# A head's queries and keys split by one wide operation per part, in a fused two-layer decoder kernel on one Trainium2 core

## Chip, core and metric

The kernel runs on one core of one Trainium2 chip, in one launch. The metric is the device time of that launch in microseconds. Three runs of the kernel before gave 3035.72, 3030.76 and 3033.51 us, median 3033.51 us.

## What is computed

Two layers over a sequence of 2048 tokens of width 1024. Layer 0 is a gated linear recurrence next to a pooling mixer. Layer 1, in which the change lies, is causal attention with 16 heads of 64, query and key normalisation and a cumulative forget bias. The part of the reference that matters:

```python
q = rms_norm(hd(q), qnorm_g); k = rms_norm(hd(k), knorm_g)
cumf = jnp.cumsum(log_sigmoid(fl + b_f), axis=1)
logits = q @ k.T * scale + cumf[query] - cumf[key]     # per head, causal
probs = softmax(where(mask, logits, -inf))
o = (probs @ v) * silu(g)
```

## The kernel before, in words

The sequence is cut into four segments of 512 tokens (`s` = 0 to 3). For each segment layer 0 runs, then layer 1. Products are made accurate by splitting operands into a rounded high part (fp32r) and the remainder, the low part; a product of two split operands takes the three terms high·high, high·low, low·high.

In layer 1, `quad_attention` (L1207) goes over the heads. For head `h` it runs `attend(s, h)`, 4(s+1) blocks of 128 keys: scores `pst` (L1148, L1149), two exponentials on ScalarE (L1153, L1154), the low part `pl` on VectorE (L184), values `pov` and `pol`. Between these blocks it runs `max_pass(s, h+1)` (L1091), which finds each query's largest score for the next head from products `pmx` (L1100), and writes it as one row of that head's `Q3` (L1114). After a head's blocks, `prep(s, h+2)` (L1059) makes the operands of the head after next. There are 64 calls of `prep`, one per segment and head. Projections of later heads (`pqk`, `pv`, `pgt`) are woven in as filling for TensorE.

`prep` transposes the normalised queries and keys of one head into one PSUM tile `pt` (named pqkT): queries on rows 0 to 63, keys on rows 64 to 127. From it come four operand tiles of 128 rows and 512 columns:

- `Q3` rows 0 to 63: high query; rows 64 to 79: constants from DRAM (`q4d`, L1079), one of which `max_pass` later overwrites with the maximum
- `K2` rows 0 to 63: high key; rows 64 to 79: forget bias from DRAM (`cfd`, L1080)
- `Q1`: high query on the lower rows, low query on the upper; `K1`: low key on the lower, high key on the upper

The scores are K1ᵀQ1 + K2ᵀQ3. `max_pass` needs only `Q3` and `K2`; `attend` needs all four, one head later. For s < 3, `K1` and `K2` are also stored to DRAM (L1082, L1083) for later segments, by the queue of SyncE (SP); weight loads (`raw`, L290) and loads of old keys and values (L1088, L1138, L1141) go through the same queue. The two loads of constants are issued from ScalarE's queue. An issue in an engine's queue that waits for a semaphore holds what stands behind it.

The order of instructions on each engine is set when the program is built: a scheduler takes instructions by priority (nearly the order in the source) when it reckons them ready. Each engine then runs its list strictly in order.

Of the kernel before, what the change touches and what calls it, by code (L numbers as in the profile page):

```python
# [12 lines left out]
AF = mybir.ActivationFunctionType  # L13
ALU = mybir.AluOpType
# [21 lines left out]
def trunk(ctx, tc, x, cvec, norm_g, ada_c, ada_w, ada_b, ada_bg, lbp, w0, w0o, w1, w1f, w1o,  # L36
          onorm, poolw, pscale, foxb, qkg, out):
    nc = tc.nc
    V, S, G = nc.vector, nc.scalar, nc.gpsimd
# [4 lines left out]
    def transpose(o, i):  # L44
        return nc.tensor.transpose(o, i, ident[0:i.shape[0], 0:i.shape[0]])
# [25 lines left out]
    def ps_misc(name):  # L71
        return ps.tile([P, 512], F32, name=name, tag="mx", bufs=2)

    def ps_pj(name):
        return ps.tile([P, 512], F32, name=name, tag="pj", bufs=2)
# [13 lines left out]
    def f(ap):  # L89
        return ap.bitcast(F32)  # L90
# [133 lines left out]

    def need(L, key, fill):
        while key not in L and fill.step():
            pass
        assert key in L, key

# [70 lines left out]
    def next_w(key, ahead=True):  # L300
        n = wpos[0]
        assert wseq[n] == key, (wseq[n], key)
        prep_w(n)
        if ahead:
            prep_w(n + 1)
        wpos[0] += 1
        return wready.pop(n)
# [203 lines left out]
    def hgrn_qf(s, h):  # L511
        L = seg0[s]
        wt, act = next_w(("a", QF[h])), L["act"]
        pq = ps_pj("pq")
        first = s == 0 and h == 0
        if first:
            pf = ps_pj("pf")
            yield from proj_T2((pq, pf), wt, act)
        else:
            yield from proj_T(pq, wt, 0, act)  # L520
        qT = qp.tile([P, SEG], F32, name="qT", tag="qa")
        S.copy(qT, pq)
        yield
        if not first:
            pf = ps_pj("pf")
            yield from proj_T(pf, wt, P, act)
        e1, e2 = tmp("e1"), tmp("e2")
        S.activation(e1, pf, AF.Exp, scale=-1.0)
        S.activation(e2, pf, AF.Exp)
        S.activation(e1, e1, AF.Ln, bias=1.0)  # L530
        S.activation(e2, e2, AF.Ln, bias=1.0)
        S.activation(e1, e1, AF.Exp, scale=-1.0)
        kT = qp.tile([P, SEG], F32, name="kT", tag="qb")
        S.activation(kT, e2, AF.Exp, scale=-1.0)
        V.tensor_scalar(kT, kT, oml[:, h:h + 1], None, op0=ALU.mult)
        S.activation(e1, e1, AF.Ln, scale=oml[:, h:h + 1], bias=lb[:, h:h + 1])
        cT = kp.tile([P, SEG], F32, name="cT", tag="k1c")
        for c in range(NTB):
            V.tensor_tensor_scan(cT[:, c * P:(c + 1) * P], e1[:, c * P:(c + 1) * P],
                                 zero1.to_broadcast([P, P]), 0.0, op0=ALU.add, op1=ALU.add)  # L540
        L["qkc", h] = (qT, kT, cT)
        yield
# [515 lines left out]

    def prep(s, h):  # L1059

        L = seg1[s]
        qk = L["qk", h // 2]
        j = h % 2
        pt = ps_misc("pqkT")
        for tb in range(NTB):
            transpose(pt[:, tb * P:(tb + 1) * P], qk[:, tb, j * P:(j + 1) * P])
        lo, up = slice(0, HD), slice(HD, P)
        g = col["qkg"]
        Q1 = qp.tile([P, SEG], F32R, name="Q1", tag="qa")
        Q3 = qp.tile([P, SEG], F32R, name="Q3", tag="qb")  # L1070
        K1 = kp.tile([P, SEG], F32R, name="K1", tag="k1c")
        K2 = kp.tile([P, SEG], F32R, name="K2", tag="k2c")
        S.activation(Q1[lo], pt[lo], AF.Copy, scale=g[lo])
        S.activation(K1[up], pt[up], AF.Copy, scale=g[up])
        V.scalar_tensor_tensor(Q1[up], pt[lo], g[lo], f(Q1[lo]), op0=ALU.mult, op1=ALU.subtract)
        V.scalar_tensor_tensor(K1[lo], pt[up], g[up], f(K1[up]), op0=ALU.mult, op1=ALU.subtract)
        S.copy(Q3[lo], f(Q1[lo]))  # L1077
        S.copy(K2[lo], f(K1[up]))
        nc.scalar.dma_start(f(Q3[HD:KX]), q4d)  # L1079
        nc.scalar.dma_start(f(K2[HD:KX]), cfd[h, :, s * SEG:(s + 1) * SEG])  # L1080
        if s < NSEG - 1:
            nc.sync.dma_start(k1d[h, :, s * SEG:(s + 1) * SEG], f(K1))  # L1082
            nc.sync.dma_start(k2d[h, :, s * SEG:(s + 1) * SEG], f(K2[0:KX]))  # L1083
        L["ops", h] = (Q1, Q3, K1, K2)
# [122 lines left out]
    def quad_attention(s, quad, fill):  # L1207

        L = seg1[s]
        nb = NTB * (s + 1)  # L1210
        for h in range(4 * quad, 4 * quad + 4):
            nxt = max_pass(s, h + 1) if h + 1 < NH else iter(())
            next(nxt, None)
            need(L, ("v", h // 2), fill)
            if h > 0 and h % 2 == 0:
                need(L, ("g", (h - 1) // 4), fill)
            for i, _ in enumerate(attend(s, h)):
                if i < nb - 2:
                    next(nxt, None)
                if i == nb // 2:  # L1220
                    next(nxt, None)
                if i == 0 and h > 0:
                    finish(s, h - 1)
                yield
            run(nxt)
            if h + 2 < NH:
                need(L, ("qk", h // 2 + 1), fill)
                prep(s, h + 2)

    def layer1(s, xs):  # L1230
# [10 lines left out]
        vq = v_quad(s, 0, ("c", 1))  # L1241
        next(vq)
        prep(s, 0)
        next(vq)
        prep(s, 1)

        fill = Steps()
# [140 lines left out]
```

## Time and profile before

| | us |
|---|---|
| runs | 3035.72, 3030.76, 3033.51 |
| median | 3033.51 |
| profiled execution, its own time | 3029.48 |
| its span, first to last instruction | 3027.8 |
| mean granted TensorE clock | 0.975 |

The profile gives, for one execution, each engine's busy time, the chain of waits that ended last, and every instruction with its line, its tiles and the idle time of its engine before it. PE is TensorE, PEld its weight loads, DVE VectorE, ACT ScalarE, POOL GpSimd, SP SyncE (which only issues transfers). A small q behind an engine means its sequencer. Tile numbers are left out, so `Q<-pqkT` at L1073 is the write of `Q1`, and at L1077 `Q<-Q` the copy into `Q3`.

### The profile page before, as it was taken

What the parts mean: (1) busy time and instruction counts of PE and PEld (TensorE: products, weight loads), DVE (VectorE), ACT (ScalarE), POOL (GpSimd) and SP (SyncE); (2) the same over time, 40 slices, a digit from 0 to 9 for tenths busy, and PEclk for the clock granted to TensorE, in tenths of its full rate; (3) what the DMA queues carried; (4) which work ended last, traced back from release to release, by engine and by line L of the source; (5) the groups of instructions that cost most, each with busy time, mean ns of one, the idle gap of its engine ahead of it and who ended that gap; (6) DMA issues with size and microseconds to landing.
All of it is one profiled execution on the core that took longest, in us unless ns stands there. A gap on an engine that the chain in (4) does not pass through costs nothing.

```text
span 3027.8 us, 49244 instructions
## 1 busy us (share of the span) xinstructions
PE 2808.9 (93%) x17212; PEld 2390.2 (79%) x17212; DVE 2301.3 (76%) x4390; ACT 1826.4 (60%) x3743; POOL 1172.5 (39%) x992
## 2 busy tenths in 40 slices
PE   4699999989999999989999999998999999999998
PEld 3688887879888887868878887776898877777777
DVE  8667678776676788886586788889667678888886
ACT  3344566774445666775455676768635467777774
POOL 3111233323211444444212355554432136566665
PEclk9899999999999999999999999999999999999999
DMA  7523365534233444533333443553342334333442
GB/s 246 174 57 102 106 141 139 119 91 124 79 102 110 119 119 104 131 99 115 100 95 116 122 124 115 126 133 113 97 126 71 114 104 115 105 113 107 113 138 86
DMA packets 207888, 348.97 MB, mean 115 GB/s; under 512 B 24068, under 2 KB 70788, under 8 KB 205080
## 3 DMA queue, kind: packets, MB, share of 16 engines
q1 hardware_dynamic: 201816, 329.03, 39.0%
q10 hardware_dynamic: 5824, 16.79, 1.7%
q8 instruction: 137, 2.24, 0.3%
q14 instruction: 111, 0.91, 0.1%
HBM read 293.58 MB, written 52.14 MB: 114 GB/s over the span
## 4 chain that ended last, share of the span: by engine, by line
PE 60%; DVE 19%; ACT 11%; DMA 4%; issue 4%; POOL 1%; SPq 0%; ACTq 0%; DVEq 0%; POOLq 0%
PE py L42 10%; PE pgt L42 8%; PE pqk L42 8%; PE pst L42 6%; PE pv L42 6%; PE pmx L42 4%; PE pov L42 3%; PE pol L42 3%; PE pf L42 3%; PE pq L42 3%; PE pl L42 3%; DVE pl L184 2%; DVE wt L184 2%; ACT wt L295 1%; DMA raw<-in_w_dram 1%
## 5 line engine op out<-in xcount | busy, mean ns | idle before, releaser
L184 POOL TENSOR_TENSOR wt<-raw,wt 128x512 fp32r<-128x512 f32 x287 | 419.5, 1470 | 1030.9 <-ACT wt L295 975.1
L1164 POOL TENSOR_TENSOR la<-la,ph 128x512 f32<-128x512 f32 (+3 forms) x528 | 610.6, 1156 | 385.7 <-ACT ph L1153 342.9
L184 DVE TENSOR_TENSOR pl<-pst,ph 128x512 fp32r<-128x512 f32 (+3 forms) x640 | 386.9, 605 | 133.4 <-ACT pst L1154 102.2
L1153 ACT ACTIVATE ph<-pst 128x512 fp32r<-128x512 f32 (+3 forms) x640 | 340.6, 532 | 235.1 <-PE pst L42 224.9
L42 PE MATMUL pqk<-wt,h 128*128 128x256 f32 x3072 | 433.1, 286 | 5.5 <-DVE h L497 2.7
L42 PEld LDWEIGHTS pqk<-wt,h 128*128 128x128 f32 x3072 | 411.9, 192 | 25.2 <-DVE h L497 3.5
L42 PE MATMUL pgt<-h,wt 128*128 128x512 f32 x1536 | 403.9, 405 | 0.0
L295 ACT CAST wt<-raw 128x512 fp32r<-128x512 f32 x578 | 335.2, 621 | 74.9 <-PE py L42 33.3
L42 PE MATMUL pv<-wt,h 128*128 128x256 f32 x2304 | 345.0, 298 | 10.7 <-DVE h L184 6.6
L42 PEld LDWEIGHTS pv<-wt,h 128*128 128x128 f32 x2304 | 326.1, 204 | 28.9 <-DVE h L184 9.6
L42 PEld LDWEIGHTS pgt<-h,wt 128*128 128x128 f32 x1536 | 293.1, 194 | 63.2 <-issue 1.9
L1154 ACT ACTIVATE pst<-pst 128x512 f32<-128x512 f32 (+3 forms) x640 | 340.0, 531 | 0.0
L184 DVE TENSOR_TENSOR wt<-raw,wt 128x512 fp32r<-128x512 f32 x291 | 265.7, 918 | 73.4 <-ACT wt L295 71.9
L1102 DVE TENSOR_REDUCE mxs<-pmx 128x1 f32<-128x512 f32 x384 | 258.6, 684 | 20.3 <-PE pmx L42 17.2
L42 PE MATMUL py<-wt,o 128*128 128x256 f32 x1536 | 202.2, 286 | 1.4 <-ACT o L1200 1.2
L42 PE MATMUL py<-wt,mix 128*128 128x256 f32 x1536 | 198.2, 287 | 2.3 <-DVE yt L844 2.1
L42 PEld LDWEIGHTS py<-wt,o 128*128 128x128 f32 x1536 | 192.8, 192 | 6.7 <-ACT o L1200 1.5
L42 PEld LDWEIGHTS py<-wt,mix 128*128 128x128 f32 x1536 | 187.9, 191 | 9.8 <-issue 4.5
L42 PE MATMUL pst<-Q,K1o 128*128 128x512 f32 x384 | 162.6, 424 | 23.2 <-DVE pl L184 21.7
L42 PE MATMUL pmx<-K2o,Q 67*128 67x512 f32 x384 | 162.0, 426 | 21.9 <-ACT Q L1077 10.2
L42 PE MATMUL pov<-ph,Vo 128*128 128x512 f32 x384 | 162.8, 425 | 6.6 <-ACT ph L1153 6.2
L1104 DVE CUSTOM_DVE_ANT_0 pmx<-pmx,mq 128x128 f32<-128x128 f32 (+3 forms) x256 | 124.6, 497 | 55.6 <-PE pmx L42 53.8
(251 smaller groups left out, 5309.1 us busy)
## 6 DMA issues: line engine op xcount, KB each, us to landing
raw<-in_w_dram SPq DMA_DIRECT2D x448, 256.0 KB, 3.5
K2o<-k2d SPq DMA_DIRECT2D x192, 160.0 KB, 3.4
Vo<-vd SPq DMA_DIRECT2D x96, 260.0 KB, 2.7
K1o<-k1d SPq DMA_DIRECT2D x96, 256.0 KB, 3.4
raw<-in_w1o_dram SPq DMA_DIRECT2D x66, 256.0 KB, 3.6
raw<-in_w0o_dram SPq DMA_DIRECT2D x64, 256.0 KB, 3.2
vd<-Vc SPq DMA_DIRECT2D x48, 260.0 KB, 8.1
ada<-in_ada_w_dram ACTq DMA_DIRECT2D x12, 1024.0 KB, 5.0
```

The source lines that it names most:

```text
L42: return nc.tensor.matmul(*a, **k)
L184: (eng or V).tensor_tensor(out_t, full, f(hi), op=ALU.subtract)
L295: S.copy(wt[:, 0, sl, :], raw)
L1102: V.tensor_reduce(mxs[:, i, c:c + 1], pm[:, 0:n], axis=AX.X, op=ALU.max)
L1104: V.tensor_tensor_reduce(pm[:, 0:n], pm[:, 0:n], mq[:, SEG - n:], 1.0, NEG, op0=ALU.add, op1=ALU.max, accum_out=mxs[:, i, c:c + 1])
L1153: S.activation(ph[:, q0:], st[:, q0:], AF.Exp)
L1154: S.activation(st[:, q0:], st[:, q0:], AF.Exp)
L1164: G.tensor_tensor(la[:, q0:], la[:, q0:], f(ph[:, q0:]), op=ALU.add)
```

## The change

Only `prep` changes, and its instructions stand one line lower from L1074 on.

```diff
-        S.activation(Q1[lo], pt[lo], AF.Copy, scale=g[lo])
-        S.activation(K1[up], pt[up], AF.Copy, scale=g[up])
-        V.scalar_tensor_tensor(Q1[up], pt[lo], g[lo], f(Q1[lo]), op0=ALU.mult, op1=ALU.subtract)
-        V.scalar_tensor_tensor(K1[lo], pt[up], g[up], f(K1[up]), op0=ALU.mult, op1=ALU.subtract)
-        S.copy(Q3[lo], f(Q1[lo]))
-        S.copy(K2[lo], f(K1[up]))
+        S.activation(Q3, pt, AF.Copy, scale=g)
+        V.scalar_tensor_tensor(Q1, pt, g, f(Q3), op0=ALU.mult, op1=ALU.subtract)
+        nc.sync.dma_start(f(K1[lo]), f(Q3[up]))
+        S.copy(K2[lo], f(Q3[up]))
+        S.copy(K1[up], f(Q1[up]))
+        S.copy(Q1[up], f(Q3[lo]))
         nc.scalar.dma_start(f(Q3[HD:KX]), q4d)
         nc.scalar.dma_start(f(K2[HD:KX]), cfd[h, :, s * SEG:(s + 1) * SEG])
```

One wide activation (now L1074) writes the high parts of query and key into the two halves of `Q3`, one wide VectorE operation (L1075) the low parts into `Q1`. The high key goes to `K1`'s lower rows by a transfer from SP's queue (L1076) and to `K2` by a copy (L1077); the low key is copied to `K1`'s upper rows (L1078), and only then the high query over it to `Q1`'s upper rows (L1079). The `q4d` rows (now L1080) overwrite rows 64 to 79 of `Q3`, on which the high key stood, so that load now waits for the transfer and the copy that read them. `Q1` and `K1` hold their parts on swapped rows, and their product is the same.

ScalarE's queue around the `prep` of segment 1, head 9. The tiles of that head are `Q1_12458`, `Q3_12459`, `K1_12460` and `K2_12461`; `ph` and the second `pst` are exponentials, `lh` and `wt` copies of other work. Before:

```order
L1079 DMA Q3_12459<-q4d_175 16x512
L1153 ACTIVATE ph_12427<-pst_12423 128x128
L1154 ACTIVATE pst_12423<-pst_12423 128x128
L1114 ACTIVATE Q3_12168<-pmt_12447 1x512
L1175 COPY u_12147<-pov_12188 64x512
L1073 ACTIVATE Q1_12458<-pqkT_12453,c_qkg_513 64x512
L1074 ACTIVATE K1_12460<-pqkT_12453,c_qkg_513 64x512
L1180 CAST lh_12443<-la_12187 128x512
L1077 CAST Q3_12459<-Q1_12458 64x512
L1078 CAST K2_12461<-K1_12460 64x512
L1080 DMA K2_12461<-cfd_174 16x512
L1153 ACTIVATE ph_12490<-pst_12487 128x512
```

With the change:

```order
L1074 ACTIVATE Q3_12459<-pqkT_12453,c_qkg_513 128x512
L295 CAST wt_12524<-raw_12525 128x512
L1181 CAST lh_12443<-la_12187 128x512
L1077 CAST K2_12461<-Q3_12459 64x512
L1078 CAST K1_12460<-Q1_12458 64x512
L1154 ACTIVATE ph_12490<-pst_12487 128x512
L1079 CAST Q1_12458<-Q3_12459 64x512
L1080 DMA Q3_12459<-q4d_175 16x512
L1155 ACTIVATE pst_12487<-pst_12487 128x512
L295 CAST wt_12524<-raw_12529 128x512
```

The `q4d` load has moved from ahead of the activation to behind all the copies, with the second exponential of a block directly behind it.

TensorE's list at the same place, from the end of that head's transposes (`pqkT`) to its first `pmx`; `pgt` is filling. Before:

```order
L45 MATMUL pqkT_12453<-ident_85,qk_11629 128x128
L42 MATMUL pst_12487<-Q1_12167,K1o_12481 128x512
L42 MATMUL pst_12487<-Q3_12168,K2o_12483 128x512
L42 MATMUL pgt_12541<-h1_9560,wt_12215 128x512 x9
L42 MATMUL pmx_12475<-K2o_12473,Q3_12459 128x512
```

With the change:

```order
L45 MATMUL pqkT_12453<-ident_85,qk_11629 128x128
L42 MATMUL pst_12487<-Q1_12167,K1o_12481 128x512
L42 MATMUL pst_12487<-Q3_12168,K2o_12483 128x512
L42 MATMUL pgt_12541<-h1_9560,wt_12215 128x512 x12
L42 MATMUL pst_12554<-Q1_12167,K1o_12481 128x512
L42 MATMUL pst_12554<-Q3_12168,K2o_12483 128x512
L42 MATMUL pov_12479<-ph_12490,Vo_12485 128x512
L42 MATMUL pgt_12541<-h1_9560,wt_12215 128x512 x10
L42 MATMUL pst_12566<-Q1_12167,K1o_12481 128x512
L42 MATMUL pmx_12475<-K2o_12473,Q3_12459 128x512
```

The first `pmx` has moved behind 28 matmuls where 11 stood before; over the 64 heads the median goes from 22.5 to 49 (matmuls of 256 or 512 columns).

SP's queue at the same place, with the change; before, the store L1082 stood directly behind the load `Vo`:

```order
L1142 DMA Vo_12753<-vd_173 128x520
L1076 DMA K1_12460<-Q3_12459 64x512
L1084 DMA k2d_172<-K2_12461 80x512
L1083 DMA k1d_171<-K1_12460 128x512
L290 DMA raw_12767<-in_w1_dram 128x512
```

The new transfer stands in the place of the store, and the two stores follow it.

## Rows read from the trace of the kernel before

**Rows 1.** The page: busy time by engine, and the chain that ended last.
```profile
PE 2808.9 (93%) x17212; PEld 2390.2 (79%) x17212; DVE 2301.3 (76%) x4390; ACT 1826.4 (60%) x3743; POOL 1172.5 (39%) x992
...
PE 60%; DVE 19%; ACT 11%; DMA 4%; issue 4%; POOL 1%; SPq 0%; ACTq 0%; DVEq 0%; POOLq 0%
```

**Rows 2.** Waits of PE, whole span: for whom, us in total, times, longest.
```profile
PE pst L42 <- DVE pl L184: 35.1, 31, 2.4
...
PE pmx L42 <- ACT Q L1077: 10.2, 19, 1.5
...
PE pmx L42 <- DVE K L1076: 4.2, 8, 0.8
...
PE pmx L42 <- DMA K<-cfd: 2.9, 1, 2.9
...
PE pmx L42 <- ACT K L1074: 2.2, 2, 1.8
...
PE pmx L42 <- ACT K L1078: 1.4, 7, 0.2
```

**Rows 3.** The compute lines of `prep`: duration in ns min/median/max, first and last start.
```profile
L1073 ACT ACTIVATE Q<-pqkT,c_qkg x64: 662/682/687, 370.2 to 2942.1; 64x512 fp32r<-64x512 f32 x64
...
L1075 DVE SCALAR_TENSOR_TENSOR Q<-pqkT,c_qkg,Q x64: 743/744/746, 372.1 to 2943.6; 64x512 fp32r<-64x512 f32 x64
...
L1076 DVE SCALAR_TENSOR_TENSOR K<-pqkT,c_qkg,K x64: 754/755/757, 374.2 to 2944.4; 64x512 fp32r<-64x512 f32 x64
...
L1077 ACT CAST Q<-Q x64: 612/620/624, 372.1 to 2943.5; 64x512 fp32r<-64x512 f32 x64
```

**Rows 4.** Two stretches of attention: length, busy us (and count) by engine, granted clock, DMA share.
```profile
core 0: us, PE busy (x) PEld busy (x) DVE busy (x) ACT busy (x) POOL busy (x), PEclk, DMA share, GB/s
1189.00:1215.00 26.00, 23.32 (x108) 17.45 (x107) 23.91 (x40) 17.84 (x38) 10.68 (x9) 0.93 0.30 93
2076.00:2107.00 31.00, 27.04 (x155) 20.65 (x154) 29.46 (x60) 27.24 (x60) 16.01 (x13) 1.00 0.42 124
```

**Rows 5.** Timeline of the `prep` of segment 1, head 9, and after it.
```profile
1187.00 0.28 PE L45 MATMUL pqkT<-ident,qk 128*128 128x128 f32 x1
...
1187.71 2.23 PE L42 MATMUL pgt<-h,wt 128*128 128x512 f32 x9
1187.94 0.68 ACT L1073 ACTIVATE Q<-pqkT,c_qkg 64x512 fp32r<-64x512 f32 x1
1187.99 0.68 DVE L1177 TENSOR_TENSOR u<-pov,u 64x512 f32<-64x512 f32 x1
...
1189.36 0.62 ACT L1180 CAST lh<-la 128x512 fp32r<-128x512 f32 x1
...
1190.55 0.50 PE L42 MATMUL pmx<-K2o,Q 67*128 67x512 f32 x1 [0.61 <-ACT Q L1077]
...
1191.16 0.60 ACT L1153 ACTIVATE ph<-pst 128x512 fp32r<-128x512 f32 x1
...
1201.82 1.01 PE L42 MATMUL pst<-Q,K 128*128 128x512 f32 x2 [2.07 <-DVE pl L184]
```

**Rows 6.** From issue to landing: the `q4d` load (L1079), then the store of `K1` (L1082, 256 KB).
```profile
L1079 ACTq DMA_DIRECT2D Q<-q4d x64: 308/308/335, 244.2 to 2938.8; - x64
...
DMA to landing us min/median/max: 1.7/2.6/4.5
...
L1082 SPq DMA_DIRECT2D k1d<-K x48: 319/326/420, 375.0 to 2111.2; - x48
L1082 SPq EVENT_SEMAPHORE  x45: 17/4657/11694, 375.0 to 2101.6; - x45
...
DMA to landing us min/median/max: 2.3/2.6/4.4
```

**Rows 7.** The SP queue's own waits: for whom, us in total, times, longest.
```profile
SPq L1082 <- DVE K L1076: 246.2, 40, 11.7
```

## The prediction

> **What bounds the kernel now.** I read the busy times first [rows 1]. TensorE is busy 93% of the span, VectorE 76%, ScalarE 60%; the chain that ended last is 60% TensorE, 19% VectorE, 11% ScalarE. So time can only be won where TensorE stands idle, and lost where it is made to.
>
> The waits of TensorE come second [rows 2]. Its largest wait in attention is for VectorE's `pl`: 35.1 us in 31 waits. Its waits for `prep` itself, at the first `pmx` of a head, are 10.2, 2.2 and 1.4 us for ScalarE's part, 4.2 for VectorE's and 2.9 for the `cfd` rows: 20.9 us in 37 waits.
>
> Third, stretches of attention [rows 4]. In 1189 to 1215 us VectorE is busy 23.91 of 26 us (92%) and TensorE 23.32; in 2076 to 2107 us, where little filling is left, VectorE has 29.46 of 31 us (95%), ScalarE 27.24 and TensorE 27.04. There VectorE is as much the bound as TensorE, unlike over the whole span. The timeline of one head shows it [rows 5]: the transposes of `prep` end at 1187.28 us, the first `pmx` waits 0.61 us at 1190.55 us, and at 1201.82 us TensorE has stood 2.07 us because VectorE is late with `pl`.
>
> **The change part by part.**
>
> *VectorE.* One operation of two goes. By [rows 3] L1075 takes 744 ns and L1076 755 ns on 64 rows and 512 columns. The wide one has the same columns on 128 rows; on ScalarE a copy of 128 rows takes 0.62 us (L1180) [rows 5] and one of 64 rows 0.62 us (L1077) [rows 3], so I price it by the columns, at 0.75 us. VectorE loses 64 × 0.755 = 48.3 us. What of it is on the path: VectorE stands in the chain for 19% of 3027.8 = 575 us, of 2301.3 us busy, a quarter; 48.3 / 4 = 12 us. Ends: nothing, if `pl` is late for other reasons, and 31 waits for `pl` × 0.755 = 23 us, one operation off each. I take −12.
>
> *ScalarE.* Before: 2 × 0.682 + 2 × 0.620 = 2.60 us a head. Now 0.682 + 3 × 0.620 = 2.54 us. 64 × 0.06 = 4 us less; ScalarE has 40% idle, so I count nothing.
>
> *The first `pmx`.* Here the path gets longer. Before, `Q3` was complete after two activations, one other copy and one copy, and its `q4d` rows had been loaded beforehand. Now those rows are loaded last. In the order shown ScalarE has seven instructions ahead of that issue, the wide activation first: 0.68 + 6 × 0.61 = 4.35 us. Over all 64 heads it is five to nine, 3.1 to 5.5 us by these durations, median 4.35. The load then takes 2.6 us to land (1.7 to 4.5) [rows 6]. So `Q3` is ready 4.35 + 2.6 = 7.0 us after the activation starts, which for this head is 1187.94 + 7.0 = 1194.9 us. TensorE in the new order has between the transposes and that `pmx` 22 `pgt` at 2.23 / 9 = 0.25 us [rows 5] and six others at about 0.25: 28 × 0.25 = 7.0 us, so from 1187.28 it arrives at about 1194.3 to 1194.6, if the `pov` among them, which waits for the later exponential, costs some tenths. The wait is 0.3 to 0.6 us, against 0.61 before. So the move of `pmx` by 17 matmuls pays for the longer path, and I count no change for this term. Ends: all 20.9 us vanish if the loads land in 1.7 us; and if half the loads land at the longest, 4.5 us instead of 2.6, 32 × 1.9 = +61 us.
>
> The Trainium skill, SBUF — State Buffer, section The DMA setup-cost knee, says that every transfer pays about 2 us whatever its size, plus its bytes over 436 GB/s. As an estimate from that page the `q4d` load of 32 KB would land in 2.1 us, each `pmx` would be ready 0.5 us earlier, and this term would be about −20 us; the trace's median is 2.6 us, and the sum keeps it.
>
> *The transfer of the high key.* It is issued from SP when the wide activation ends, at 0.7 us, and lands 2.6 us later (2.3 to 4.4), by the store of `K1`, twice its size [rows 6]: at 3.3 us. The `q4d` issue comes up at 4.35 us, so ScalarE does not stand for it, unless landing takes over 4.35 − 0.7 = 3.6 us. SP must be there in time: before, it stood at the store of `K1` for a median of 4.66 us a wait, 246.2 us in all [rows 6, 7], so it was early, and the new transfer has the store's place. In segment 3, where there was no store, SP now waits too, with loads of old keys behind it, but only until the activation is done. Nothing for this, with +6 us as the other end (16 heads × 0.4).
>
> *The new wait of ScalarE for VectorE* (L1078 needs the low part). The low part can start at 0.7 us and end at 1.45; in the head shown VectorE is first done with `u` at 1188.67 [rows 5], 0.73 after the start, so nothing is lost. ScalarE comes to L1078 after 2.4 us at the median. Behind it stand exponentials. Nothing, if VectorE is not over 1 us behind.
>
> *Where filling is short.* In 7 heads near the ends of segments the new order has only 11 to 25 matmuls ahead of the first `pmx`, some 3 us against 7.0 ready. But these are stretches like 2076 to 2107 us, where TensorE has 4 us idle anyway. At most 7 × 4 = 28 us; I take +2.
>
> *The sum.* −12 + 0 + 0 + 2 = −10 us. On the profiled execution, 3029.48 us, that is 3019.5; its time lies 4.0 us under the median of the runs, so for a median I forecast 3033.51 − 10 = **3023.5 us**. The forecast's own range is 3008 to 3029.
>
> **The rivals.**
>
> *1. The first `pmx` comes late (slower).* Two transfers now stand one behind the other ahead of it, and a late `Q3` also holds the `pst` behind that `pmx` on TensorE. It decides where the load's landing exceeds 2.6 us by more than the slack of nothing to 0.3 us. For it: half the loads land later than 2.6 us, up to 4.5 [rows 6], and these are loads that nothing waited for. Against: TensorE has 7.0 us of other work there. Price: between 64 × 0.5 = 32 and 61 us, less the 12 won: 3033.5 + 20 to + 49, at the middle 3068 us.
>
> *2. ScalarE stands at its own queue (slower).* It waits for VectorE at L1078 or for the transfer at the `q4d` issue, and the exponentials behind are late. In the trace before, ScalarE's queue never held a load on a transfer just issued. The Trainium skill, DMA: Bandwidth & Descriptors, section Anatomy of one DMA, says that the DMA engines wait on no semaphore: the issuing sequencer does, ahead of dispatch; no row here shows such a hold on ScalarE, and by that rule the hold would be ScalarE's. If the landing takes 4.4 us [rows 6], it holds 0.8 us a head, 51 us of ScalarE in all. By ScalarE's 11% of the chain 6 us of that are on the path, and if a third of it is, since exponentials stand right behind, 17 us. Against the 12 won that is 3028 to 3039, about 3036 us.
>
> *3. VectorE's work was cover (no change).* The 48 us sit beside TensorE's filling and only move idle time. For it: TensorE has 93% and the same matmuls remain. Against: the 35.1 us of waits for `pl`. Then 3033 us.
>
> *4. More than forecast (faster).* The later `pmx` also moves its maxima on VectorE out of the crowded start of a head. All 35.1 us of the waits for `pl` go: 3033.5 − 35 = 2998 us.
>
> **How the numbers follow.** A measurement of this kernel can tell about 0.2%, 6 us. Forecast 0.38, rival 4 0.12, rival 3 0.18, rival 1 0.22, rival 2 0.10. Faster by over 0.2% is the forecast and rival 4: 0.50. Within 0.2%: rival 3 and part of rival 2: 0.21. Slower: rival 1 and the rest of rival 2: 0.29. The range goes from 2999 (rival 4's end) to 3066, about the middle of rival 1, and leaves out some 2 in 10.
>
> **What would show it.** Right: VectorE busy about 48 us less, with 64 wide operations of about 0.75 us at L1075; the wait of `pst` for `pl` down from 35.1 us towards 20; TensorE's wait at `pmx` for the `q4d` rows about 20 us in all; almost no hold of ScalarE at L1080. Rival 1: a wait of `pmx` for the `q4d` load of 1 us or more a head. Rival 2: long semaphore rows on ScalarE's queue at L1078 or L1080, and waits of TensorE for exponentials above what they are now. The forecast is wrong if the wait for `pl` stays at 35 us, or if the wide VectorE operation takes much over 0.75 us.

## The result, and the profile after

The change made the kernel slower. Four runs of it gave 3068.91 to 3082.71 us, median 3075.68, and four of the kernel before 3030.76 to 3037.74, median 3034.61: a ratio of 1.0138, 95% interval 1.0119 to 1.0158. That is 41 us more, where 10 us less were forecast. The profiled execution took 3076.22 us, its span is 3074.5 us, and its mean granted TensorE clock is 0.969 (before 0.975).

The page of the changed kernel, busy time and chain:

```profile
PE 2823.8 (92%) x17212; PEld 2395.1 (78%) x17212; DVE 2233.3 (73%) x4326; ACT 1826.5 (59%) x3743; POOL 1166.3 (38%) x992
...
PE 56%; DVE 16%; ACT 13%; DMA 9%; issue 4%; POOL 1%; SPq 0%; ACTq 0%; DVEq 0%; POOLq 0%
```

Against [rows 1], VectorE has 68 us less to do and leaves part of the chain, 19% to 16%. What enters it are transfers: 4% to 9%. TensorE makes the same 17212 matmuls, but is busy 14.9 us longer, and its idle time (span less busy) grows from 218.9 to 250.7 us, by 31.8. Both together are the 46.7 us between the two spans.

The lines of `prep` with the change, by line (ns min/median/max, first and last start), with the landing of the two transfers:

```profile
L1074 ACT ACTIVATE Q<-pqkT,c_qkg x64: 663/689/697, 372.3 to 2987.6; 128x512 fp32r<-128x512 f32 x64
...
L1075 DVE SCALAR_TENSOR_TENSOR Q<-pqkT,c_qkg,Q x64: 731/750/753, 373.0 to 2988.9; 128x512 fp32r<-128x512 f32 x64
...
L1076 SPq DMA_DIRECT2D K<-Q x64: 461/467/527, 373.0 to 2988.3; - x64
...
  ACT junk L457: 7.4, 2
  ACT pst L1155: 4.9, 4
...
DMA to landing us min/median/max: 2.2/2.2/3.8
...
L1080 ACTq DMA_DIRECT2D Q<-q4d x64: 308/314/385, 375.3 to 2990.6; - x64
L1080 ACTq EVENT_SEMAPHORE  x58: 17/17/3146, 378.3 to 2990.3; - x58
...
DMA to landing us min/median/max: 1.7/1.9/4.3
```

Every duration came out as priced: 0.75 us for the wide VectorE operation, 0.69 for the wide activation. The two rows of ScalarE under L1076 are idle times that the transfer ended (us, times); with four smaller ones they are 20.7 us. The landing rows look harmless, but the view found a landing for only some of the issues (28 of the 64 `q4d` loads, 17 of the 64 transfers; in [rows 6] 17 of 64 loads), and the timelines below show longer ones. The `q4d` load went out a median of 3.2 us after the activation began, where 4.35 were forecast: 0.7 us to the transfer's issue, 2.2 to its landing, and the load right behind.

The waits of TensorE with the change (for whom, us in total, times, longest):

```profile
PE pov L42 <- ACT ph L1154: 31.9, 38, 3.5
...
PE pst L42 <- DVE pl L184: 20.8, 37, 1.4
PE pst L42 <- DMA K2o<-k2d: 19.8, 13, 3.7
...
PE pmx L42 <- DVE mxs L1103: 12.0, 23, 1.8
PE pmx L42 <- DMA Q<-q4d: 11.6, 8, 6.1
...
PE pmx L42 <- DMA vd<-Vc: 5.4, 1, 5.4
```

The same view of the kernel before, beyond what stands in [rows 2]:

```profile
PE pov L42 <- ACT ph L1153: 8.0, 13, 2.2
...
PE pmx L42 <- DVE mxs L1102: 2.0, 2, 1.5
...
PE pst L42 <- DMA K2o<-k2d: 1.2, 2, 1.0
```

The wait for `pl` fell from 35.1 us [rows 2] to 20.8, as foretold. The waits for exponentials (+23.9), old keys (+18.6), maxima (+10.0) and the `q4d` load (+11.6) are what came. The wait of 5.4 us put down to `vd<-Vc` is that of the first `pmx` of head 12, which reads no v; the `q4d` load of that head had been issued 9.3 us before it ended.

Where in the program? I took the time from the end of one head's transposes to the next's, for all 64 calls of `prep` (numbered 0 to 63, 16 to a segment), and subtracted before from after. About half of the heads became a little faster. Heads 4, 8 and 12 of segments 0 to 2, each the first of a group of four, lost 47.0 us together (numbers 4, 12, 28, 36 and 40 each 7.3 to 9.0), and the nine heads behind them won 16.3 back. Segment 3 lost 11.2 us, where neither kernel stores v. Ahead of and in those nine heads `v_quad` (L1047 to L1049) sends four stores of v to DRAM through SP's queue. These heads are not the whole of it, and not all of their loss is that of the late `pmx`: the version of experiment 7, which has neither the transfer nor the late load and is faster than before, loses 22.2 us in the same nine heads, where loads of old keys come late. Against the version of experiment 1, which differs from the change by the transfer alone, the change loses 20.6 us in the nine heads and those behind them, and 26.7 us in all the others. These are differences of single executions, and the time of the kernel before alone differs by 7 us among its four runs.

Head 4, in segment 0, shows the late load most clearly. A timeline with the change (start, us, engine, line, and in brackets the idle time before):

```profile
446.08 0.60 PE L45 MATMUL pqkT<-ident,qk 128*128 128x128 f32 x4
...
448.14 0.69 ACT L1074 ACTIVATE Q<-pqkT,c_qkg 128x512 fp32r<-128x512 f32 x1
...
448.86 0.47 SPq L1076 DMA_DIRECT2D K<-Q  x1
...
450.14 1.06 SPq L1049 DMA_DIRECT2D vd<-Vc  x2
...
452.03 0.33 SPq L1083 DMA_DIRECT2D k1d<-K  x1
...
452.10 0.32 ACTq L1080 DMA_DIRECT2D Q<-q4d  x1
...
461.29 0.80 PE L42 MATMUL pmx<-K,Q 67*128 67x128 f32 x2 [6.09 <-DMA Q<-q4d]
```

The transfer of the high key was issued 0.7 us after the activation began and the `q4d` load at 4.0 us, near the 4.35 forecast. But the load then took 9.2 us to let `pmx` start: 461.29 − 452.10. In the kernel before, the same head's transposes began at 443.44 us, and its first `pmx` waited 0.21 us:

```profile
448.24 0.33 PE L42 MATMUL pmx<-K,Q 67*128 67x128 f32 x1 [0.21 <-ACT K L1078]
```

What the DMA engines did from 444 to 463 us with the change (busy tenths in 40 slices; then issues: count, KB each, median us to landing):

```profile
DMA  6951000980003898999999799999899999999999
...
vd<-Vc SPq DMA_DIRECT2D x4, 260.0 KB, 8.8
...
k1d<-K SPq DMA_DIRECT2D x1, 256.0 KB, 9.4
```

From the issues at 450.14 us on they are busy in nine tenths of nearly every slice, with four stores of v ahead of or beside the `q4d` load and weight loads of 256 and 512 KB behind it; the store of `K1` issued next to it, at 452.03 us, took 9.4 us, against a median of 2.6 [rows 6].

Head 12 looks the same. In segments 1 and 2 it is the transfer that is late. Head 4 of segment 2, number 36, has two stores ahead of it (the same view):

```profile
1791.53 0.92 SPq L1049 DMA_DIRECT2D vd<-Vc  x2
...
1793.98 0.69 ACT L1074 ACTIVATE Q<-pqkT,c_qkg 128x512 fp32r<-128x512 f32 x1
...
1794.69 0.47 SPq L1076 DMA_DIRECT2D K<-Q  x1
...
1800.00 0.36 ACTq L1080 DMA_DIRECT2D Q<-q4d  x1
1800.03 0.32 SPq L1083 DMA_DIRECT2D k1d<-K  x1
...
1800.41 0.58 ACT L1155 ACTIVATE pst<-pst 128x512 f32<-128x512 f32 x1 [1.75 <-DMA K<-Q]
...
1801.02 0.69 DVE L184 TENSOR_TENSOR pl<-pst,ph 128x512 fp32r<-128x512 f32 x1 [3.92 <-ACT pst L1155]
...
1802.42 0.73 PE L42 MATMUL pmx<-K2o,Q 67*128 67x512 f32 x2
```

The `q4d` load and the store of `K1`, which both wait for the transfer, go off at the same moment, 5.3 us after its issue; ScalarE stands 1.75 us at its own queue, VectorE 3.92 us for the exponential behind it. The first `pmx` comes 8.4 us after the activation. At the six such heads of segments 1 and 2 `q4d` is issued 5.7 to 8.4 us after the activation (median of all heads 3.2); the first `pmx` then waits for it at two of them, 1.3 and 0.5 us. What this costs at numbers 36 and 40 is not shown: the version of experiment 7 loses 6.8 and 7.3 us there too, with waits of 5.0 us each for old keys.

At head 4 the idle time was followed by a lower clock. Two stretches there, ahead of the wait and behind it (length, busy us by engine, then granted clock, DMA share, GB/s):

```profile
446.70:455.00 8.30, 7.68 (x60) 6.92 (x59) 6.50 (x12) 8.10 (x17) 3.79 (x4) 1.00 0.76 151
461.30:467.80 6.50, 6.50 (x28) 5.96 (x29) 4.97 (x13) 1.62 (x4) 0.65 (x2) 0.50 0.61 173
```

TensorE worked at 2.4 GHz, stood idle for 6.09 us, and then had 1.2 GHz for the whole next stretch. By the mean granted clocks of the two executions (0.975 of 3027.8 us, 0.969 of 3074.5) 1.2 GHz was granted for an estimated 40 us more in the changed kernel, which fits the 14.9 us of longer busy time. What head 4 lost did not last: before, the `pmx` at head 5 waited 2.9 us for `cfd` [rows 2] with a lower clock around it, and heads 4 and 5 together took 41.6 us before and 41.8 with the change. Head 12 with the one behind it kept 7.2 us, number 28 with its follower 7.0.

### The profile page after: what moved, and what is told of

The parts are those of the page before. It is cut to its first block, busy times and chain, and to the rows that moved or that the text cites. A ratio compares the mean times of both kernels' runs of the same rounds, so it can differ in the third digit from the quotient of the medians.

```text
span 3074.5 us, 49203 instructions
## 1 busy us (share of the span) xinstructions
PE 2823.8 (92%) x17212; PEld 2395.1 (78%) x17212; DVE 2233.3 (73%) x4326; ACT 1826.5 (59%) x3743; POOL 1166.3 (38%) x992
## 4 chain that ended last, share of the span: by engine, by line
PE 56%; DVE 16%; ACT 13%; DMA 9%; issue 4%; POOL 1%; SPq 0%; ACTq 0%; DVEq 0%; POOLq 0%
PE py L42 9%; PE pgt L42 8%; PE pqk L42 6%; PE pst L42 6%; PE pv L42 4%; PE pov L42 3%; PE pmx L42 3%; PE pol L42 3%; PE pf L42 3%; PE pq L42 3%; PE pl L42 2%; DMA K<-Q 2%; DMA raw<-in_w_dram 2%; DMA K2o<-k2d 2%; ACT wt L295 2%
## 5 line engine op out<-in xcount | busy, mean ns | idle before, releaser
L184 POOL TENSOR_TENSOR wt<-raw,wt 128x512 fp32r<-128x512 f32 x287 | 413.2, 1447 | 1036.7 <-ACT wt L295 981.0
L1154 ACT ACTIVATE ph<-pst 128x512 fp32r<-128x512 f32 (+3 forms) x640 | 341.6, 534 | 250.7 <-PE pst L42 239.5
L42 PE MATMUL pqk<-wt,h 128*128 128x256 f32 x3072 | 442.4, 287 | 5.6 <-DVE h L497 2.6
L42 PEld LDWEIGHTS pqk<-wt,h 128*128 128x128 f32 x3072 | 418.5, 194 | 26.8 <-DVE h L497 3.4
L42 PE MATMUL pv<-wt,h 128*128 128x256 f32 x2304 | 336.6, 293 | 8.4 <-DVE h L184 4.9
L42 PEld LDWEIGHTS pv<-wt,h 128*128 128x128 f32 x2304 | 316.9, 199 | 25.9 <-DVE h L184 7.4
L42 PEld LDWEIGHTS py<-wt,mix 128*128 128x128 f32 x1536 | 187.9, 191 | 11.6 <-issue 4.5
L42 PE MATMUL pst<-Q,K2o 67*128 67x512 f32 x384 | 161.0, 423 | 22.4 <-DMA K2o<-k2d 19.8
L42 PE MATMUL pmx<-K2o,Q 67*128 67x512 f32 x384 | 155.6, 429 | 16.1 <-DVE mxs L1103 10.6
```

The lines of the kernel that those rows point to most:

```text
L42: return nc.tensor.matmul(*a, **k)
L184: (eng or V).tensor_tensor(out_t, full, f(hi), op=ALU.subtract)
L1154: S.activation(ph[:, q0:], st[:, q0:], AF.Exp)
```

## The experiments

Theory A: the first `pmx` is late, because the transfer and then the `q4d` load stand one behind the other ahead of it and both get slow beside the stores of v. Rival B: ScalarE's queue, held at L1080, makes exponentials late. Rival C: the later load alone does it, with or without a transfer. Rival D: the transfer costs by being there, on SP's queue and on the DMA engines. Ratios are to the kernel before, run on the same chip beside each.

**1. No transfer** (against the change):

```diff
-        nc.sync.dma_start(f(K1[lo]), f(Q3[up]))
+        S.copy(K1[lo], f(Q3[up]))
```

> The changed kernel with the high key moved to K1 by a ScalarE copy instead of the transfer; the q4d load still comes last. Theory T (what costs the 41 us are the two transfers that now stand one behind the other ahead of a head's first pmx: at the first head of each quarter of the heads in segments 0 to 2 they queue behind the stores of v, land in 5 us or more, hold ScalarE at the q4d issue, and pmx comes late): no hold at the q4d issue is left, about half the loss goes, 3050 us (3040 to 3060), with waits of pmx for q4d left over. Rival F (the cost is the longer path itself: pmx stands behind twice the filling, which is then missing elsewhere, wherever the transfers land): the path is as long, 3070 us or more. Rival S (ScalarE's longer chain of copies and its wait for VectorE delay the exponentials): one copy of 0.62 us more a head, 3080 to 3110 us.

Measured: 3028.90 us, ratio 1.0016 (0.9999 to 1.0032). A ScalarE copy in place of the transfer takes away nearly the whole loss, though ScalarE has 64 copies more and `q4d` is still loaded after them, a median of 2.5 us after the activation starts (3.2 with the change). On that chip this is 5 us over the kernel before, just under the 6 to 26 that theory T gave, and far from F and S. So the loss of the change goes with its transfer; a late load issued at 2.5 us alone doesn't carry it. The waits of TensorE here:

```profile
PE pst L42 <- DMA K2o<-k2d: 13.2, 13, 2.9
...
PE pov L42 <- ACT ph L1154: 12.6, 19, 2.4
...
PE pmx L42 <- DMA Q<-q4d: 9.6, 5, 2.9
```

The waits for exponentials fall from 31.9 to 12.6 us, but the nine heads with stores of v still lose 21.7 us, with waits for `q4d` and for old keys.

**2. The transfer kept, off the path to `pmx`** (against before: a tile `H` of their own for the high parts, so that the `q4d` rows are loaded early again):

```diff
+        H = tmp("H", F32R)
+        S.activation(H, pt, AF.Copy, scale=g)
+        V.scalar_tensor_tensor(Q1, pt, g, f(H), op0=ALU.mult, op1=ALU.subtract)
+        S.copy(Q3[lo], f(H[lo]))
+        S.copy(K2[lo], f(H[up]))
+        nc.sync.dma_start(f(K1[lo]), f(H[up]))
+        S.copy(K1[up], f(Q1[up]))
+        S.copy(Q1[up], f(H[lo]))
```

> The changed kernel with the high parts in a tile of their own, from which Q3, K2, K1 (still by the transfer) and Q1 are filled, so that the q4d load can be issued ahead of everything again. One ScalarE copy more a head (40 us of ScalarE in all). Theory T: nothing waits for the transfer any more before the next head, no hold, pmx early: 3020 to 3035 us, at or below the kernel before. Rival F: the path is short again, also 3020 to 3035 us. Rival S: 3085 us or more, since ScalarE has more to copy than in the changed kernel.

Measured: 3035.33 us, ratio 1.0041 (1.0029 to 1.0053). The first `pmx` comes a median of 2.26 us after the activation starts (6.88 with the change, 2.73 before), and two thirds of the loss are gone. That is 11 us over the kernel before on that chip, where T and F expected next to none. In its trace numbers 36 and 40 lose 6.9 and 7.0 us, with waits of 4.6 and 4.8 us for old keys.

**3. The transfer from ScalarE's queue** (against the change):

```diff
-        nc.sync.dma_start(f(K1[lo]), f(Q3[up]))
+        nc.scalar.dma_start(f(K1[lo]), f(Q3[up]))
```

> The changed kernel with the transfer issued from ScalarE's queue instead of SP's, so that it stands behind no store or load of SP's queue. Theory T, where the queueing is in SP's own queue: the transfer lands in 2.2 us at every head, the holds at the q4d issue go, 3040 to 3055 us. Theory T, where the sixteen DMA engines themselves are full of the stores of v: landing stays 5 us at those heads, 3070 to 3080 us. Rivals F and S: no change from the changed kernel, 3075 us.

Measured: 3055.48 us, ratio 1.0115 (1.0084 to 1.0146). Standing behind the stores on SP's queue is at most a small part of it; the first `pmx` is nearly as late as with the change, 6.76 us. The result lies between the two expected for theory T, so how much is SP's queue and how much the DMA engines stays open.

**4. A late load without a transfer** (against before: the activation that makes `Q3` also writes its rows 64 to 79, so that `q4d` must follow it; those values are overwritten):

```diff
-        S.copy(Q3[lo], f(Q1[lo]))
+        S.activation(Q3[0:KX], pt[0:KX], AF.Copy, scale=g[0:KX])
```

> The kernel before (two narrow VectorE operations, no transfer) with one thing altered: Q3's activation also writes the rows of q4d, with values that the load then overwrites, so the q4d load has to come after it. Theory T: one load on the path instead of two transfers, no hold of ScalarE; a few heads where the load lands late: 3040 to 3055 us. Rival F: pmx has to be put behind more filling, and VectorE has both its operations: 3065 to 3090 us. Rival S: nothing new on ScalarE, 3035 us.

Measured: 3105.19 us, ratio 1.0277 (1.0249 to 1.0306). It was not the clean test that I wanted: the scheduler put this activation late, behind VectorE's reading of the same PSUM tile, as the row of that line in the by-line view shows, and the first `pmx` came a median of 8.51 us after the first activation.

```profile
L1077 ACT ACTIVATE Q<-pqkT,c_qkg x64: 667/683/687, 376.4 to 3021.7; 80x512 fp32r<-80x512 f32 x64
its engine sat idle before it (us, times) until:
  DVE K L1076: 9.5, 13
```

None of the three expectations came. It shows that a late load can go with a loss of 2.8% without any transfer between tiles. That the lateness itself is what is paid for is likely, taken with experiment 1, but not shown: this edit also makes the activation at L1077 a reader of the PSUM tile and holds that tile longer. A late load that is issued at 2.5 us, as in experiment 1, is early enough at most heads.

**5. The `q4d` load from SP's queue** (against the change), which takes the hold at L1080 off ScalarE:

```diff
-        nc.scalar.dma_start(f(Q3[HD:KX]), q4d)
+        nc.sync.dma_start(f(Q3[HD:KX]), q4d)
```

> The changed kernel with the q4d load issued from SP's queue instead of ScalarE's: it waits for the transfer there, and ScalarE never stands for it. If ScalarE's hold (some 16 us in all in the changed kernel, at a few heads) and the late exponentials behind it are the larger part of the loss: +15 to +25 us against the kernel before. If the late landing of what pmx needs is the larger part: +35 to +45 us, since the load comes no earlier. Rival F: +40 us.

Measured: 3080.42 us, ratio 1.0160 (1.0122 to 1.0198): no gain, and a little more than the 45 us expected at most. So B is not what decides: the hold of ScalarE at heads like number 36 is real, but with the load moved to SP's queue, which now stands for it instead, the waits of TensorE for exponentials only fall from 31.9 to 23.7 us, the first `pmx` comes hardly earlier, a median of 6.71 us after the activation against 6.88, and `pmx` waits longer for `q4d` than with the change, 15.4 us against 11.6.

**6. The stores of v spread out**, with the change and, as a control, in the kernel before. The loop at L1047 to L1049 goes, and each head stores its own v in the middle of its blocks, after GpSimd has written its column of ones once more (that only makes the store wait until then):

```diff
+                    if s < NSEG - 1:
+                        vj = L["v", h // 2][:, :, h % 2, :]
...
+                        nc.sync.dma_start(vd[h, :, s * NTB:(s + 1) * NTB, :], f(vj))
```

> The changed kernel, with each head's store of v issued in the middle of that head (the column of ones is written again from a value of that block, so that the store cannot go earlier) instead of four stores together at the end of a projection, which in the changed kernel fall on the first prep of a quarter. Theory T (the transfer and the q4d load queue behind those stores): against the kernel before, +0 to +15 us instead of the changed kernel's +41, and the first heads of the quarters in segments 0 to 2, where the changed kernel lost 47 us, lose under 15. Rival F (the longer path to pmx costs wherever things land): +35 to +45 us as in the changed kernel.

> The control for the spread stores: the kernel before with the same spreading. Theory T and rival F alike: nothing in the kernel before waits for a transfer that was just issued, so within 10 us of it. Only the difference between the two runs with spread stores tells the theories apart.

Measured: the change with spread stores 3037.53 us, ratio 1.0019 (1.0000 to 1.0039); before with spread stores 3021.01 us, ratio 0.9966 (0.9950 to 0.9982). Spreading is worth 0.34% without the change and 1.2% with it, so some 0.85% of the change's 1.38% are its meeting with the bundled stores. Against its own control the change still loses 1.0019/0.9966 = 1.0053. The nine heads lose 14.9 us against the trace before, just under the 15 of theory T, and 18.5 against that of the control. The control itself gained more than the 10 us that were expected to bound it: spreading the stores pays without the change too.

**7. GpSimd moves the half tiles** (as experiment 2, with no transfer and the three moves on GpSimd):

```diff
-        nc.sync.dma_start(f(K1[lo]), f(H[up]))
-        S.copy(K1[up], f(Q1[up]))
-        S.copy(Q1[up], f(H[lo]))
+        G.tensor_copy(K1[lo], f(H[up]))
+        G.tensor_copy(K1[up], f(Q1[up]))
+        G.tensor_copy(Q1[up], f(H[lo]))
```

> The wide operations alone, without a transfer and with the q4d load early: high parts in a tile of their own, Q3 and K2 filled by two ScalarE copies, and the three half tiles that are only needed a head later moved by GpSimd (some 115 us more there, 39% busy). ScalarE has 43 us less than before, VectorE 48 us less. By my forecast's term for VectorE: 12 us below the kernel before. If VectorE's operation was only cover: within 6 us of it. If GpSimd's sums of the probabilities, which share its queue, come late: above it.

Measured: 3023.60 us, ratio 0.9977 (0.9960 to 0.9994). With neither a transfer nor a late load, and the moves on GpSimd, the wide operations do win, 7 us by the ratio. How much of that is VectorE's and how much the copies that ScalarE no longer makes, this run does not tell. TensorE waits for old keys here as well (1.2 us before):

```profile
PE pst L42 <- DMA K2o<-k2d: 16.8, 8, 5.0
```

**8. Versions 1, 7 and 2 with spread stores** (the edit of experiment 6 in each):

> The change with a ScalarE copy in place of its transfer, and each head's store of v moved to the middle of the next-but-one stretch of work as in e7. If what e7 still loses against e8 (about 0.53%, 16 us) is the transfer itself, which makes the first pmx of every head 4 us later, this kernel falls to e8's ratio, 0.997 +- 0.002. If it is the late load of the low query parts, which this kernel still has (issued 2.5 us after the activation), it stays near e7, 1.002.

> e3 (wide operations, a tile of their own for the high parts, no transfer, the load of the low query parts early, three half tiles moved by GpSimd) with the spread stores of v. If the two gains add, 0.9977 times 0.9966 = 0.994. If both come from the same waits at the first heads of each quarter, no better than e8, 0.997.

> e2 (transfer kept but off the path to the first pmx, one more ScalarE copy) with the spread stores of v. If e2's loss (1.0041) is ScalarE's added copy, 64 times 0.5 us and more behind VectorE, it stays above e8 by as much as e2 above before: 1.0007. If it came from the transfer beside the stores of v, it falls to e8's 0.997 or under.

Measured: with the copy 3008.79 us, ratio 0.9934 (0.9910 to 0.9958); with GpSimd **3001.15 us, ratio 0.9908 (0.9883 to 0.9933)**; with the transfer off the path 3021.58 us, ratio 0.9977 (0.9962 to 0.9992). All kernels side by side:

| form of `prep` | stores of v bundled | spread | spread, against the control |
|---|---|---|---|
| before | 1 | 0.9966 | 1 |
| the change | 1.0138 | 1.0019 | 1.0053 |
| copy in place of the transfer | 1.0016 | 0.9934 | 0.9968 |
| transfer off the path, early `q4d` | 1.0041 | 0.9977 | 1.0011 |
| GpSimd moves, early `q4d` | 0.9977 | 0.9908 | 0.9942 |

The last column is the quotient of two ratios, in the three lower rows from different chips, so good to some 0.003. The copy with spread stores came out lower than expected, and so did GpSimd with spread stores (0.9908, where the two gains added give 0.994). The copy and the change, both with spread stores, differ by 0.85%, and both load `q4d` late: so what the change still loses there goes with the transfer. The waits of TensorE, first in the change with spread stores, whose profiled execution is the longest of its ten (3049.56 us) and where line numbers are three lower, then in the version with the copy:

```profile
PE pov L42 <- ACT ph L1151: 24.8, 36, 2.3
...
PE pmx L42 <- DVE mxs L1100: 14.5, 25, 1.7
...
PE pmx L42 <- DMA Q<-q4d: 3.3, 6, 0.9
```

```profile
PE pov L42 <- ACT ph L1151: 13.2, 21, 2.4
...
PE pmx L42 <- DVE mxs L1100: 4.8, 13, 0.7
```

Nearly nothing waits for `q4d` at the first `pmx` any more, yet the waits for exponentials and maxima stay in the first, and are a half and a third of that in the second. In these two programs TensorE has a median of 49 and of 43.5 matmuls between a head's transposes and its first `pmx` (22.5 before), and comes to it 6.86 and 5.61 us after the activation starts. This is consistent with filling being used up ahead of `pmx`, so that the maxima and the blocks of the head are crowded behind it; no run separates that order from the delay itself.

The fastest version is the one with GpSimd and spread stores. Its page and waits:

```profile
PE 2796.1 (93%) x17212; PEld 2383.2 (79%) x17212; DVE 2253.6 (75%) x4326; ACT 1770.6 (59%) x3679; POOL 1321.7 (44%) x1232
```

```profile
PE pst L42 <- DVE pl L184: 24.8, 26, 2.2
...
PE pov L42 <- ACT ph L1153: 3.8, 10, 1.4
...
PE pst L42 <- DMA K2o<-k2d: 3.2, 5, 1.0
```

GpSimd takes on some 150 us that it had free, ScalarE loses 56, and TensorE's idle time is 201.9 us.

**9. A transfer that nobody waits for** (against version 1 with spread stores):

```diff
+        D = tmp("D", F32R)
+        nc.sync.dma_start(f(D[lo]), f(K2[lo]))
```

> e10 (ScalarE copy for the high key, spread stores of v, ratio 0.9934) with one added transfer a head of the same size, from the same queue (SP), out of K2's high key into a spare tile that nothing reads. If the transfer costs by being there (the load on the DMA engines, and SP's queue standing for it with weight loads behind), the ratio rises towards e7's 1.0019 or at least e12's 0.9977. If it costs only where the first pmx waits behind it and the load of the low query parts, the ratio stays at 0.9934, within its interval.

Measured: 3012.57 us, ratio 0.9946 (0.9928 to 0.9964), against 0.9934 without it; the two intervals overlap. The row of this transfer, with its waits on SP's queue:

```profile
L1076 SPq EVENT_SEMAPHORE  x87: 17/28/6847, 375.3 to 2915.1; - x87
L1076 SPq DMA_DIRECT2D D<-K x64: 467/467/937, 375.3 to 2922.0; - x64
...
DMA to landing us min/median/max: 2.2/2.3/3.3
```

D falls: 64 such transfers, with SP standing for up to 6.8 us ahead of one, cost some 0.1%, which this measurement can't tell from nothing. What costs is that work waits for the transfer. The waits of TensorE for exponentials are longer here than without the spare transfer (21.0 us against 13.2) at nearly the same time, so such a row is a sign and not a price.

## Why the prediction was wrong

**VectorE: right in the work, not shown in the time.** 64 operations of 0.755 us went, the wide one takes 0.75 us, and the wait for `pl` fell to 20.8 us, a little more than the −12 that the sum took. Whether it wins 12 us no run isolates: the copy with spread stores is 0.32% under its control, 10 us, but that quotient is good to some 0.3% only, and in experiment 7 the copies moved too. The other 20 us that VectorE lost are changes of the durations of other lines, which I didn't follow up.

**ScalarE: right.** 1826.5 us against 1826.4 [rows 1].

**The first `pmx`, counted at nothing: this step failed.** The time of the median came out, in part by luck: 7.0 us from activation to a ready `Q3` were forecast, and the first `pmx` came after 6.88. But at the median the load went out at 3.2 us instead of 4.35, and the known landings took 1.9 us instead of 2.6, so that `Q3` was ready at some 5.1 us; what set the 6.88 were the 49 matmuls ahead. What failed is, first, the median landing of 2.6 us, put in for every head. In [rows 6] those were loads that were issued 2.45 us (median) ahead of the activation and that nothing waited for, with a longest of 4.5 us. The change moves them into the stretch behind the activation, and at the first heads of a group that is where the stores of v of 260 KB run. There, but for head 8 of segment 0, the first `pmx` came 7.6 to 13.3 us after the activation, behind transfers of 5 to 9 us, and spreading those stores takes away 0.85% of the 1.38% (experiment 6). The upper end, +61, allowed for 4.5 us at half the heads. Secondly, the sentence "the move of `pmx` by 17 matmuls pays for the longer path" treats filling as free. It paid at the first `pmx` of most heads, whose waits for `q4d` are 11.6 us in all, 17 with that of head 12. The waits for exponentials and maxima then rose by 34 us, which fits filling that is missing behind `pmx`; that this is the cause stays open.

**The transfer of the high key, counted at nothing: this step failed too.** It landed in 2.2 us at the median, but in 5.3 at number 36, over the 3.6 us that the text gave as the point from which ScalarE stands. And the bound of +6 us looked only at whom it holds on a queue; as the first of two transfers in a row ahead of `pmx` it carries nearly the whole loss: with a ScalarE copy in its place the ratio is 1.0016 instead of 1.0138 (experiment 1), and one that nobody waits for costs next to nothing (experiment 9). The Trainium skill, SBUF — State Buffer, section The DMA setup-cost knee, with its fixed 2 us and bytes over 436 GB/s, fits a quiet stretch here: the `q4d` load landed in 1.7 us at the least and 1.9 at the median. No term of it covers the 5.3 and 9.2 us beside the stores of v.

**ScalarE's new wait: right**, 5.3 us in 14 waits at L1078. **Short filling, +2: not isolated.** Segment 3, which has none of the stores, lost 11.2 us with the change, but the version of experiment 1 won 3.3 us there, so that loss goes with the transfer as well.

**The rivals.** Rival 1 named the late `pmx` behind two transfers, and its 3068 us lie near the 3075.68, though it priced a wait at the load and no old keys; the range stopped at its middle. The sign that I gave for it, a wait of 1 us or more a head at `q4d`, did not come; the lateness shows mostly one step on, behind `pmx`. Rival 2 happens, for 20.7 us of ScalarE's time (of the 51 in its text), but moving it to SP's queue gains nothing (experiment 5). By the rule cited for it (the Trainium skill, DMA: Bandwidth & Descriptors, section Anatomy of one DMA) the hold is ScalarE's and not the DMA engines', and the trace agrees: the semaphore row at L1080 reaches 3.1 us. Of the 35 us in rival 4, 14 came at `pl`, though not by its mechanism: the waits for maxima rose.

Open: why the version with the transfer off the path and an early `q4d` (0.9977) doesn't reach the copy with a late one (0.9934). In its trace the wait for `pl` is 33.8 us against 25.0, but no run isolates that.

## What to carry to other kernels

A transfer that was issued early and waited for by nobody tells nothing of what it costs when it is put on the path: look at what the DMA engines carry in the stretch to which it moves, head by head, and price the worst stretch, not the median. Filling that hides a longer path may be borrowed from the work behind it, so look for the loss there too. Compare the place of a loss with a version that lacks the suspected cause: numbers 36 and 40 lost 7 us each without any late load. Rows can be swapped by an engine with free time (here GpSimd) at less risk than by a transfer, and a bundle of stores is worth spreading for its own sake.

## What the hardware showed that was not expected

- Loads of the same 32 KB from the same queue took 1.9 us (median of the known landings) and 9.2 us, the latter beside four stores of 260 KB and weight loads. A store of 256 KB took 9.4 us there and 2.6 at its median before.
- A single idle time of TensorE of 6.09 us was followed by 6.5 us at a granted clock of 0.50. Over the whole span TensorE was busy 14.9 us longer with the same matmuls, half of what its idle time grew by (31.8 us).
- Moving 64 half tiles of 128 KB each by transfer costs about nothing where nobody waits (0.9946 against 0.9934) and 0.85% where the first product of a head does.
